# Attention scores as products of high and low parts, the rotated dimensions stacked on 128 rows

## The chip, the cores and the metric

The kernel runs on one core of a Trainium2 chip. The metric is the time of one execution in device microseconds (us). The core has a matrix engine (PE, with its weight loads PEld), a vector engine (DVE), an activation engine (ACT), a general engine (POOL), and a queue of its own for transfers (SP). Each engine works through its instructions in a fixed order and waits on semaphores for the others.

## The reference, cut to what matters

Four layers follow each other on 256 positions and 256 context positions of width 1024: a gated unit, a recurrent mixer, latent attention, and the gated unit again. The change lies in the third, the latent attention with 16 heads. A head has 128 plain dimensions and 64 rotated ones, and keys and queries are normalised over all 192:

```python
q = rms_norm((rms_norm(c_q, q_norm) @ w_uq).reshape(.., 16, 192), qk_gain_q)
k = rms_norm(concat([k_nope, broadcast(k_rope)]), qk_gain_k)      # 128 + 64
q_rot, k_rot = apply_rope(q, cos, sin), apply_rope(k, cos, sin)   # last 64 turn
s = concat([q @ k_ctx.T, q_rot @ k_rot.T])     # 256 context keys, then 256 own keys
o = softmax(s * 192 ** -0.5) @ concat([v_ctx, v])
x = x + gate * ((o * silu(z)) @ w_out)
```

So a score against a context key uses the query before its rotation, and a score against an own key the query after it.

## The kernel before, in words

Activations lie with features on the 128 partitions and positions along them. `T` is 512: context positions 0 to 255, then own positions 256 to 511.

Large products run in a one-pass format (`F32R`): each fp32 operand is split into a high part and a low part (`hi` and `lo` for weights, `x[:, 0]` and `x[:, 1]` for data), and `mm3` (L319) adds three products: high by high, high by low, low by high. A cast on ACT makes the high part (L190 and L317), a subtraction on DVE the low part (L191 and L318). Other products, the scores among them, take plain fp32 operands; the trace has two PE records for each of those.

The attention layer is the function `mla`. A scheduler sets the order on each engine; the order in which the code yields is its input.

- **Gates stage** (about 1060 to 1148 us of the span): `gates` makes 16 tiles z, one for each head; beside it run `latents` (the normalised latents, the rotated shared key `krg`) and `project(0)`.
- **Attend stage** (about 1148 to 1390 us): eight groups g of two heads each. `attend(g)` makes scores, softmax and the product with the values; `project(g+1)` runs beside it and makes the next group's keys, values and queries. From g = 5 on the first three parts of the output product run along.

In `project`, `keys` makes a head's 128 plain key rows, `scaled` multiplies them and the shared rotated key by the norm, `values` makes v, `queries` the plain query rows, `rotate` the turned query rows of both heads at once (product with a 128x128 `swap` matrix, then sine and cosine), `norms` the query norms. In `attend` a score tile `sc` of 128 queries by 512 keys takes three fp32 products (L1376 to L1378): 128 plain rows by 512 keys, 64 unrotated rows (`qo`) by the 256 context keys, 64 rotated rows (`qr`) by the 256 own keys. DVE takes the maximum, ACT the exponential, DVE scales it; PE transposes it (`pT`, L1353) half a group later and multiplies it with the values (`po`, L1358).

Weights come by `wload` (L185): a transfer into `raw`, the cast and the subtraction, with four `raw` tiles and three pairs of `hi` and `lo` in this layer.

Of the kernel before, what the change touches and what calls it, by code (L numbers as in the profile page):

```python
# [9 lines left out]
F32R = mybir.dt.float32r  # L10
AF = mybir.ActivationFunctionType
ALU = mybir.AluOpType
# [5 lines left out]
T = 512  # L18
# [18 lines left out]
def layout(inp):  # L37
# [55 lines left out]
    o["swap"] = np.kron(np.eye(2, dtype=f), sw)  # L93
# [5 lines left out]
def body(tc, I, out):  # L99
# [77 lines left out]
    def wload(src, n=None):  # L177
        return next(wparts(src, n))
# [963 lines left out]
    def mla(m):  # L1142
        with phase("2", 0, 0, 4, psum=(("pA", 4), ("pB", 4)), wn=1024, hi=3):
            ep = env["a"]

            def tl(tag, shape, bufs, dtype=F32):
                return ep.tile(list(shape), dtype, tag=tag, name=tag, bufs=bufs)
# [6 lines left out]
            swap = tl("swap", [128, 128], 1)  # L1154
# [89 lines left out]
            def rotate(dst, src):  # L1244
                p = ps("sw", "pA")
                PE.matmul(p[:, 0:256], swap, src, start=True, stop=True)
                t = tl("t1", q256, 4)
                V.tensor_tensor(t, p[:, 0:256], rope[:, 1], ALU.mult)
                V.tensor_tensor(dst, src, rope[:, 0], ALU.mult)
                V.tensor_tensor(dst, dst, t, ALU.add)  # L1250

            def project(g, d):
# [3 lines left out]
                kt = lambda: tl("hx" if g else "s", [128, T], 8 if g else 16)  # L1256
                d["krh"], d["v"] = kt(), []

                def keys(hh):
                    p = ps("kn", "pA")  # L1260
                    for k in range(2):
                        sl = slice(k * 256 + hh * 128, k * 256 + hh * 128 + 128)
                        mm3(p, w[0][:, sl], w[1][:, sl], ckv[k], k == 0, k == 1)
                    t = kt()
# [4 lines left out]
                    d["kn"].append(t)  # L1269
                    return sq  # L1270

                def scaled(hh, sq):
                    p = ps("kss", "pA")
                    PE.matmul(p, ones, sq, start=True, stop=True)
                    hf = slice(64 * hh, 64 * hh + 64)
                    r = tl("lt", [128, T], 4)
                    rsqrt_bc(r, p, 1.0 / 192, eps)
                    t = d["kn"][hh]
                    V.scalar_tensor_tensor(out=t, in0=t, scalar=vec[:, 10:11], in1=r, op0=ALU.mult, op1=ALU.mult)
                    V.tensor_tensor(d["krh"][hf], krg[hf], r[hf], ALU.mult)  # L1280
# [20 lines left out]
                scaled(0, k0)  # L1301
# [3 lines left out]
                scaled(1, k1)  # L1305
                yield
                qo, ro, qrs = tl("qo", q256, 2), tl("qr", q256, 2), tl("t1", q256, 4)
                mm256(wload(I["ml_qr"][g], 768), cq, qo)
                S.activation(qrs, qo, AF.Square)
                S.activation(qo, qo, AF.Identity, scale=vec[:, 9:10])  # L1310
                yield
                d["qo"], d["qr"], d["qn"] = qo, ro, []
                d["rq"] = rq = tl("rq", [128, 4], 2)

                def queries(hh):
                    hf = slice(64 * hh, 64 * hh + 64)
                    t = tl("qn", q256, 4)
                    mm256(wload(I["ml_qn"][g * 2 + hh], 768), cq, t)
                    sq = tl("t1", q256, 4)
                    S.activation(sq, t, AF.Square)  # L1320
                    V.tensor_tensor(sq[hf], sq[hf], qrs[hf], ALU.add)
                    S.activation(t, t, AF.Identity, scale=vec[:, 8:9])
                    d["qn"].append(t)
                    return sq
# [11 lines left out]
                rotate(ro, qo)  # L1336
                yield
                q1 = queries(1)
                norms(0, q0)
                yield  # L1340
                yield
# [24 lines left out]
            def attend(g, d, before):  # L1366

                rq = d["rq"]
                for hh in range(2):
                    hf = slice(64 * hh, 64 * hh + 64)  # L1370
                    pt = []
                    for qb in range(2):
# [3 lines left out]
                        PE.matmul(p, d["qn"][hh][:, qs], d["kn"][hh], start=True, stop=False)  # L1376
                        PE.matmul(p[:, 0:256], d["qo"][hf, qs], d["krh"][hf, 0:256], start=False, stop=False)  # L1377
                        PE.matmul(p[:, 256:512], d["qr"][hf, qs], d["krh"][hf, 256:512], start=False, stop=True)  # L1378
# [20 lines left out]
            krg = tl("krg", [128, T], 1)  # L1399

            def latents():
                yield from latent(ckvr, 6, 256, T, ckv)
                S.activation(krs, kr[0:64], AF.Square)
                S.activation(krg, kr, AF.Identity, scale=vec[:, 11:12])
                krr = tl("t1", q256, 4)
                rotate(krr, krg[:, X])
                V.tensor_copy(krg[:, X], krr)
                yield
                yield from latent(cqr, 0, 768, 256, cq)
# [67 lines left out]
```

## Time and profile before

| | |
|---|---|
| median of 3 runs | 1613.46 us (1609.02 to 1613.62) |
| profiled execution | 1612.92 us, of which the span of its instructions 1611.1 us |
| PE busy | 1519.5 us, 94% of the span |
| DVE busy | 1149.1 us, 71% |
| ACT busy | 795.2 us, 49% |

The profiled execution lies 0.54 us under the median and has 1.8 us outside its span. A share over the whole span says little here, since the four layers have different limits. How the attention layer stands is read from its own stretch: how much of it PE, DVE and ACT are busy, and whether PE had idle time there. A busy PE is not PE at its peak, because matmuls overlap; what a product costs is read from the distance between the starts of consecutive ones.

### The profile page before, as it was taken

The numbers are of one execution on the slowest core, as the hardware profiler recorded it, in microseconds if no ns is written. First come the engines' busy times: TensorE is split into PE (matmuls) and PEld (weight loads), VectorE is DVE, ScalarE is ACT, GpSimd is POOL, SyncE is SP. The second block draws the span as 40 slices with busy tenths as digits, with TensorE's granted clock in tenths as the row PEclk, the third lists the DMA queues.
The fourth block names the chain that finished last, engine by engine and source line by source line (L and its number), as shares of the span: only waits on it lengthen the run. The fifth ranks groups of instructions, "written<-read, shape, count | busy, mean of one in ns | idle before, by whom it ended". The sixth has DMA issues, their size and how long they took to land.

```text
span 1611.1 us, 29355 instructions
## 1 busy us (share of the span) xinstructions
PE 1519.5 (94%) x11860; PEld 1181.4 (73%) x11860; DVE 1149.1 (71%) x2160; ACT 795.2 (49%) x1434; POOL 101.1 (6%) x135
## 2 busy tenths in 40 slices
PE   5999999999988998999998999799999999989998
PEld 2768888888966644776776777688777777768887
DVE  3769998864898377586887844778766666665876
ACT  4534331223665354345345332569866766356543
POOL 0000000000000132303213000000000000000000
PEclk9999999999999999899999999999999999989999
DMA  9766567742144652532433133134321222265452
GB/s 352 271 246 224 191 218 260 261 153 79 53 144 150 183 164 70 153 96 74 126 99 94 62 100 121 53 118 145 115 74 53 80 85 92 70 233 199 165 183 79
DMA packets 95176, 229.07 MB, mean 142 GB/s; under 512 B 26048, under 2 KB 52160, under 8 KB 80576
## 3 DMA queue, kind: packets, MB, share of 16 engines
q1 hardware_dynamic: 92736, 223.00, 40.8%
q10 hardware_dynamic: 2304, 4.20, 0.7%
q8 instruction: 93, 1.52, 0.4%
q14 instruction: 43, 0.35, 0.1%
HBM read 208.81 MB, written 17.83 MB: 141 GB/s over the span
## 4 chain that ended last, share of the span: by engine, by line
PE 47%; DVE 7%; ACT 5%; issue 1%; POOL 1%; DMA 0%; ACTq 0%; POOLq 0%; DVEq 0%
PE fm L323 5%; PE op L323 4%; PE pg L976 3%; PE fm L324 2%; PE op L1047 2%; PE op L324 2%; PE pz L323 2%; PE pu L323 2%; PE po L1358 2%; PE sc L1376 2%; PE pe L862 2%; PE sc L1377 1%; PE pv L416 1%; PE pv L417 1%; PE pz L324 1%
## 5 line engine op out<-in xcount | busy, mean ns | idle before, releaser
L191 DVE TENSOR_TENSOR lo<-raw,hi 128x2048 fp32r<-128x2048 f32 (+3 forms) x161 | 251.7, 1567 | 108.6 <-ACT hi L190 108.1
L190 ACT CAST hi<-raw 128x2048 fp32r<-128x2048 f32 (+3 forms) x161 | 212.1, 1324 | 226.9 <-PE op L327 40.6
L258 DVE SCALAR_TENSOR_TENSOR junk<-adaw,scb 128x1024 f32<-128x1024 f32 x112 | 136.7, 1221 | 10.0 <-DMA adaw<-in_ada_wT 8.1
L323 PE MATMUL op<-s,hi 128*128 128x512 f32 x256 | 91.6, 400 | 0.0
L415 PE MATMUL pv<-hi,hp 128*128 128x512 f32 x192 | 78.2, 409 | 9.1 <-ACT hi L190 6.0
L416 PE MATMUL pv<-lo,hp 128*128 128x512 f32 x192 | 77.7, 405 | 1.7 <-DVE lo L191 1.7
L323 PE MATMUL fm<-hx,hi 128*128 128x512 f32 x200 | 74.1, 411 | 4.1 <-ACT hx L317 3.8
L417 PE MATMUL pv<-hi,hp 128*128 128x512 f32 x192 | 77.2, 402 | 0.0
L324 PE MATMUL op<-s,lo 128*128 128x256 f32 x256 | 71.1, 280 | 0.0
L976 PE MATMUL pg<-xz,wz 128*128 128x256 f32 x256 | 70.2, 408 | 0.0
L767 POOL TENSOR_TENSOR BK<-f 64x256 f32<-64x256 f32 x64 | 57.3, 895 | 44.4 <-DVE f L760 27.4
L866 DVE TENSOR_TENSOR E<-pe,masks 128x512 f32<-128x512 f32 x64 | 41.5, 682 | 25.5 <-PE pe L862 23.0
L324 PE MATMUL fm<-hx,lo 128*128 128x256 f32 x200 | 56.7, 288 | 2.0 <-DVE lo L191 2.0
L323 PEld LDWEIGHTS op<-s,hi 128*128 128x128 f32 x256 | 48.1, 188 | 12.5 <-issue 1.3
L1076 PE MATMUL pv<-wv,xv 128*128 128x512 f32 x128 | 57.2, 596 | 0.0
L1047 PE MATMUL op<-Y,wo 128*128 128x256 f32 x192 | 55.8, 427 | 1.3 <-DVE xT L1051 1.3
L323 PE MATMUL fm<-cq,hi 128*128 128x512 f32 x144 | 55.7, 422 | 0.0
L976 PEld LDWEIGHTS pg<-xz,wz 128*128 128x128 f32 x256 | 47.0, 197 | 11.5 <-issue 3.8
L415 PEld LDWEIGHTS pv<-hi,hp 128*128 128x128 f32 x192 | 37.7, 197 | 19.4 <-ACT hi L190 6.6
L326 PE MATMUL pu<-hp,hi 128*128 128x512 f32 x128 | 51.1, 400 | 0.0
L327 PE MATMUL pu<-hp,hi 128*128 128x512 f32 x128 | 50.5, 395 | 0.0
L328 PE MATMUL pz<-hp,lo 128*128 128x512 f32 x128 | 50.5, 395 | 0.0
(413 smaller groups left out, 4088.2 us busy)
## 6 DMA issues: line engine op xcount, KB each, us to landing
adaw<-in_ada_wT SPq DMA_DIRECT2D x36, 1024.0 KB, 4.9
raw<-in_sgu_v SPq DMA_DIRECT2D x16, 1024.0 KB, 4.8
raw<-in_sgu_u SPq DMA_DIRECT2D x16, 1024.0 KB, 4.8
raw<-in_sgu_z SPq DMA_DIRECT2D x16, 1024.0 KB, 4.7
raw<-in_sgu_o SPq DMA_DIRECT2D x16, 1024.0 KB, 4.8
adaw<-in_ada_w SPq DMA_DIRECT2D x24, 512.0 KB, 9.6
xz<-xz SPq DMA_DIRECT2D x32, 256.0 KB, 4.2
raw<-in_ml_z SPq DMA_DIRECT2D x16, 512.0 KB, 3.6
```

What stands on the lines that cost most here:

```text
L190: S.copy(hi[:, sl], raw[:, sl])
L191: V.tensor_tensor(lo[:, sl], raw[:, sl], hi[:, sl], ALU.subtract)
L258: V.scalar_tensor_tensor(out=junk, in0=raw[:, f, :], scalar=1.0, in1=scb[:, c, :], op0=ALU.mult, op1=ALU.mult, accum_out=m[:, t * 2 + f, c ...
L323: PE.matmul(p, whi, x, start=start, stop=False)
L324: PE.matmul(p[:, 0:256], wlo, x[:, 0], start=False, stop=stop)
L415: PE.matmul(pv[tb], hs[k][:, 0, sl], whi[:, ws_], start=k == 0, stop=False)
L416: PE.matmul(pv[tb], hs[k][:, 0, sl], wlo[:, ws_], start=False, stop=False)
L417: PE.matmul(pv[tb], hs[k][:, 1, sl], whi[:, ws_], start=False, stop=k == 7)
L767: nc.gpsimd.tensor_tensor(bk[H[h], 2 * h:2 * h + 7:2, :], k4[H[h], sg], c4[H[h], sg], ALU.mult)
L976: PE.matmul(p, ws[k // 4][:, k % 4, pr * 128:pr * 128 + 128], xs[k // 2][:, k % 2, :], start=k == 0, stop=k == 7)
L1047: PE.matmul(p[:, ob], w[:, k, ob, :], y[:, k], start=k == 0, stop=k == 1)
L1076: PE.matmul(p, xv[:, k, tb * 128:tb * 128 + 128], ws[k // 4][:, k % 4, :], start=k == 0, stop=k == 7)
```

## The change

Scores. Keys and queries of a head are kept as high and low parts, and a score tile now takes six one-pass products of 128 rows by 512 keys: three for the plain rows, three for the 64 unrotated and 64 rotated rows, which are stacked on 128 rows. For head 0 of a pair the unrotated query rows are the upper 64 and the rotated ones the lower 64; for head 1 the other way round. The key side (`krg[0]`, `krg[1]`) has zeros where an unrotated row would meet an own key or a rotated row a context key.

Rotation. `swap` becomes 128x256: its second half exchanges the two heads' rows without turning them, so that the cosine part too comes out of a product, on the rows where the stack needs it. `rotate` is now called after the second head's queries, and its result is split.

Buffers. `raw` has three tiles instead of four in this layer; the key tiles of a group are four (high and low for two heads) where they were three.

```diff
-    o["swap"] = np.kron(np.eye(2, dtype=f), sw)
+    o["swap"] = np.concatenate([np.roll(np.kron(np.eye(2, dtype=f), x), 64, 1) for x in (sw, np.eye(64, dtype=f))], 1)
...
-        with phase("2", 0, 0, 4, psum=(("pA", 4), ("pB", 4)), wn=1024, hi=3):
+        with phase("2", 0, 0, 3, psum=(("pA", 4), ("pB", 4)), wn=1024, hi=3):
...
             def rotate(dst, src):
                 p = ps("sw", "pA")
-                PE.matmul(p[:, 0:256], swap, src, start=True, stop=True)
+                for i in range(2):
+                    PE.matmul(p[:, i * 256:i * 256 + 256], swap[:, i * 128:i * 128 + 128], src, start=True, stop=True)
                 t = tl("t1", q256, 4)
                 V.tensor_tensor(t, p[:, 0:256], rope[:, 1], ALU.mult)
-                V.tensor_tensor(dst, src, rope[:, 0], ALU.mult)
-                V.tensor_tensor(dst, dst, t, ALU.add)
+                u = tl("t1", q256, 4)
+                V.tensor_tensor(u, p[:, 256:512], rope[:, 0], ALU.mult)
+                for hf, x in dst:
+                    V.tensor_tensor(x, u[hf], t[hf], ALU.add)
...
                 def scaled(hh, t, sq):
...
                     V.scalar_tensor_tensor(out=t, in0=t, scalar=vec[:, 10:11], in1=r, op0=ALU.mult, op1=ALU.mult)
-                    V.tensor_tensor(d["krh"][hf], krg[hf], r[hf], ALU.mult)
+                    x = kt(), kt()
+                    S.copy(x[0], t)
+                    V.tensor_tensor(x[1], t, x[0], ALU.subtract)
+                    d["kn"].append(x)
+                    V.tensor_tensor(r, krg[hh], r, ALU.mult)
+                    x = tl("rp", [128, 2, T], 3, F32R)
+                    split(r, x)
+                    d["kr"].append(x)
...
                 def queries(hh):
...
-                    S.activation(t, t, AF.Identity, scale=vec[:, 8:9])
-                    d["qn"].append(t)
+                    x = tl("qn", [128, 2, 256], 3, F32R)
+                    S.activation(x[:, 0], t, AF.Identity, scale=vec[:, 8:9])
+                    V.scalar_tensor_tensor(out=x[:, 1], in0=t, scalar=vec[:, 8:9], in1=x[:, 0], op0=ALU.mult, op1=ALU.subtract)
+                    d["qn"].append(x)
...
                 q0 = queries(0)
                 yield
-                rotate(ro, qo)
-                yield
+                for hh in range(2):
+                    S.copy(qo[64 * hh:64 * hh + 64, hh], qt[64 * hh:64 * hh + 64])
                 q1 = queries(1)
+                yield
                 norms(0, q0)
                 yield
+                rotate([(slice(64, 128), qo[64:128, 0]), (slice(0, 64), qo[0:64, 1])], qt)
+                d["qr"] = tl("qp", [128, 2, 2, 256], 2, F32R)
+                split(qo, d["qr"])
                 yield
                 norms(1, q1)
...
-                        PE.matmul(p, d["qn"][hh][:, qs], d["kn"][hh], start=True, stop=False)
-                        PE.matmul(p[:, 0:256], d["qo"][hf, qs], d["krh"][hf, 0:256], start=False, stop=False)
-                        PE.matmul(p[:, 256:512], d["qr"][hf, qs], d["krh"][hf, 256:512], start=False, stop=True)
+                        (kh, kl), q = d["kn"][hh], d["qn"][hh]
+                        PE.matmul(p, q[:, 0, qs], kh, start=True, stop=False)
+                        PE.matmul(p, q[:, 0, qs], kl, start=False, stop=False)
+                        PE.matmul(p, q[:, 1, qs], kh, start=False, stop=False)
+                        mm3(p, d["qr"][:, 0, hh, qs], d["qr"][:, 1, hh, qs], d["kr"][hh], False, True)
...
-                krr = tl("t1", q256, 4)
-                rotate(krr, krg[:, X])
-                V.tensor_copy(krg[:, X], krr)
+                for hh in range(2):
+                    hf, of = (slice(64 * i, 64 * i + 64) for i in (hh, 1 - hh))
+                    nc.gpsimd.memset(krg[hh][hf, X], 0.0)
+                    nc.gpsimd.memset(krg[hh][of, 0:256], 0.0)
+                    S.copy(krg[hh][hf, 0:256], kr[hf, 0:256])
+                rotate([(slice(64, 128), krg[0][64:128, X]), (slice(0, 64), krg[1][0:64, X])], kr[:, X])
```

The scheduler's order, first on PE at the end of a group's projection before the change: from the rotation of group 3 (`sw`) to the first scores that use it (`sc` from `qr`). `fm` is a query product, `kn` a key product.

```order
L1246 MATMUL sw<-qo,swap 128x256
L1353 MATMUL pT<-ident,e 128x128 x4
L323 MATMUL fm<-cq,hi 128x512
...
L324 MATMUL fm<-cq,lo 128x256
L1376 MATMUL sc<-hx,qn 128x512
L1329 MATMUL qss<-ones,t_11922 128x1 x2
L1377 MATMUL sc<-hx,qo 128x256
L1378 MATMUL sc<-hx,qr 128x256
L1358 MATMUL po<-pT,v 128x256 x4
...
L1376 MATMUL sc<-hx,qn 128x512
L1377 MATMUL sc<-hx,qo 128x256
L1378 MATMUL sc<-hx,qr 128x256
```

The same place in the changed kernel (`rp` and `qp` are the split stacked rows of keys and queries):

```order
L1249 MATMUL sw<-t_11990,swap 128x256 x2
L1374 MATMUL po<-pT,v 128x256 x4
L1392 MATMUL sc<-hx,qn 128x512
L1341 MATMUL qss<-ones,t_12088 128x1 x2
L327 MATMUL kn<-ckv,hi 128x512
...
L329 MATMUL kn<-ckv,lo 128x512
L1393 MATMUL sc<-hx,qn 128x512
L1394 MATMUL sc<-hx,qn 128x512
L327 MATMUL sc<-rp,qp 128x512
L328 MATMUL sc<-rp,qp 128x512
```

Before, a whole query product of twelve matmuls, transposes, one more score tile and a value product stand between the rotation and its first use in the next group; now a value product, two norms and one key product of six matmuls do.

On ACT, where `scaled` runs for the two heads (`lt` holds the norm), before:

```order
L286 ACTIVATE lt<-lt 128x512
L190 CAST hi<-raw 128x768
L1383 ACTIVATE e,sm<-sc,sm,rq 128x512
L1293 COPY v<-pv 128x512 x2
L317 CAST s<-z 128x256
```

and in the changed kernel (`kf` is the fp32 key, `hx` its high part):

```order
L287 ACTIVATE lt<-lt 128x512
L1283 CAST hx<-kf 128x512
L191 CAST hi<-raw 128x768
L318 CAST rp<-lt 128x512
L1302 COPY v<-pv 128x512
L1400 ACTIVATE e,sm<-sc,sm,rq 128x512
```

The cast of the scaled key stands directly behind the activation that makes the norm, with one DVE instruction between them in the data's path; the weights' cast and the exponential stand behind it.

## Rows read from the trace of the kernel before

**Rows 1.** The page's head: busy time (share of the span) of each engine.
```profile
PE 1519.5 (94%) x11860; PEld 1181.4 (73%) x11860; DVE 1149.1 (71%) x2160; ACT 795.2 (49%) x1434; POOL 101.1 (6%) x135
```
**Rows 2.** Busy time by stretch: gates stage, groups 0, 3, 5 and 7.
```profile
core 0: us, PE busy (x) PEld busy (x) DVE busy (x) ACT busy (x) POOL busy (x), PEclk, DMA share, GB/s
1090.00:1110.00 20.00, 18.29 (x102) 15.37 (x101) 19.75 (x41) 19.63 (x46) 0.00 (x0) 1.00 0.35 115
1110.00:1147.90 37.90, 37.90 (x216) 32.46 (x215) 31.67 (x57) 34.96 (x78) 0.00 (x0) 1.00 0.51 167
1147.90:1173.90 26.00, 26.00 (x128) 18.94 (x127) 18.32 (x38) 19.28 (x42) 0.00 (x0) 1.00 0.28 85
1233.20:1261.80 28.60, 28.60 (x144) 21.41 (x144) 18.17 (x38) 19.58 (x41) 0.00 (x0) 1.00 0.21 69
1288.50:1325.50 37.00, 37.00 (x191) 28.62 (x190) 24.43 (x47) 23.28 (x45) 0.00 (x0) 1.00 0.28 93
1362.60:1390.00 27.40, 27.32 (x136) 20.53 (x135) 15.18 (x35) 12.52 (x26) 0.00 (x0) 1.00 0.15 49
```
**Rows 3.** PE in order of time, a score tile and the key product behind it.
```profile
start us, us, engine line op out<-in xcount [idle before <-releaser]
1261.77 1.02 PE L1376 MATMUL sc<-hx,qn 128*128 128x512 f32 x2
...
1263.26 0.59 PE L1378 MATMUL sc<-hx,qr 64*128 64x256 f32 x2
1263.78 0.50 PE L326 MATMUL kn<-ckv,hi 128*128 128x512 f32 x1
1264.12 0.39 PE L327 MATMUL kn<-ckv,hi 128*128 128x512 f32 x1
...
1265.28 0.60 PE L1353 MATMUL pT<-ident,e 128*128 128x128 f32 x4
```
**Rows 4.** The key product's weight loads, attend stage (ns: least, median, most).
```profile
L327 PEld LDWEIGHTS kn<-ckv,hi x28: 187/188/192, 1149.2 to 1333.0; 128*128 128x128 f32 x28
```
**Rows 5.** PE in order of time, the rotation of a later group.
```profile
1281.33 0.60 PE L1246 MATMUL sw<-qo,swap 128*128 128x256 f32 x2
1281.76 0.60 PE L1353 MATMUL pT<-ident,e 128*128 128x128 f32 x4
```
**Rows 6.** ACT in order of time, gates stage.
```profile
1091.75 0.61 ACT L317 CAST ckv<-s 128x512 fp32r<-128x512 f32 x1
1092.26 0.37 ACT L1184 COPY z<-fm 128x256 f32<-128x256 f32 x1
1092.52 0.63 ACT L317 CAST ckv<-s 128x512 fp32r<-128x512 f32 x1
```
**Rows 7.** DVE in order of time, gates stage.
```profile
1094.30 0.68 DVE L318 TENSOR_TENSOR ckv<-s,ckv 128x512 fp32r<-128x512 f32 x1
1094.90 0.41 DVE L1185 TENSOR_TENSOR z<-z,fm 128x256 f32<-128x256 f32 x1
1095.23 1.22 DVE L191 TENSOR_TENSOR lo<-raw,hi 128x1024 fp32r<-128x1024 f32 x1
```
**Rows 8.** Groups of instructions, 1085 to 1390 us: ACT's waits for DVE, DVE's scaling.
```profile
L1383 ACT ACTIVATE e<-sc,sm,rq 128x512 f32<-128x512 f32 x32 | 24.8, 776 | 17.3 <-DVE sm L1381 17.3
L1309 ACT ACTIVATE t<-qo 128x256 f32<-128x256 f32 x8 | 3.3, 415 | 8.0 <-DVE qo L1185 8.0
L1320 ACT ACTIVATE t<-qn 128x256 f32<-128x256 f32 x16 | 6.7, 417 | 5.8 <-DVE qn L1185 5.8
L1279 DVE SCALAR_TENSOR_TENSOR hx<-hx,vec,lt 128x512 f32<-128x512 f32 x14 | 10.5, 752 | 18.5 <-ACT lt L286 18.2
L1280 DVE TENSOR_TENSOR hx<-krg,lt 64x512 f32<-64x512 f32 x14 | 9.6, 683 | 0.1
```
**Rows 9.** PE in order of time, the two waits in the gates stage.
```profile
1101.33 0.39 PE L324 MATMUL fm<-hx,lo 128*128 128x256 f32 x1 [0.73 <-DVE lo L191]
1105.38 0.39 PE L324 MATMUL fm<-hx,lo 128*128 128x256 f32 x1 [0.98 <-DVE lo L191]
```
**Rows 10.** Weight transfers of the gates stage.
```profile
DMA to landing us min/median/max: 2.9/3.5/4.7
```

More of the change, by code (lines that the diff above doesn't have):

```diff
@@ L1153, in mla @@
             nc.sync.dma_start(out=rope, in_=I["rope"])
-            swap = tl("swap", [128, 128], 1)
+            swap = tl("swap", [128, 256], 1)
             nc.sync.dma_start(out=swap, in_=I["swap"])
@@ L1255, in project @@
                 d["kn"] = []
-                kt = lambda: tl("hx" if g else "s", [128, T], 8 if g else 16)
-                d["krh"], d["v"] = kt(), []
+                kt = lambda: tl("hx" if g else "s", [128, T], 8 if g else 16, F32R)
+                d["kr"], d["v"] = [], []
                 def keys(hh):
@@ L1263, in keys @@
                         mm3(p, w[0][:, sl], w[1][:, sl], ckv[k], k == 0, k == 1)
-                    t = kt()
+                    t = tl("kf", [128, T], 2)
                     S.copy(t, p)
@@ L1268, in keys, with scaled @@
                     V.tensor_tensor(sq[0:64], sq[0:64], krs, ALU.add)
-                    d["kn"].append(t)
-                    return sq
-                def scaled(hh, sq):
+                    return t, sq
+                def scaled(hh, t, sq):
                     p = ps("kss", "pA")
                     PE.matmul(p, ones, sq, start=True, stop=True)
-                    hf = slice(64 * hh, 64 * hh + 64)
                     r = tl("lt", [128, T], 4)
                     rsqrt_bc(r, p, 1.0 / 192, eps)
-                    t = d["kn"][hh]
                     V.scalar_tensor_tensor(out=t, in0=t, scalar=vec[:, 10:11], in1=r, op0=ALU.mult, op1=ALU.mult)
-                    V.tensor_tensor(d["krh"][hf], krg[hf], r[hf], ALU.mult)
+                    x = kt(), kt()
[6 more added lines that the diff above has]
+                    d["kr"].append(x)
                 def values(tb):
@@ L1300, in project @@
                 yield
-                scaled(0, k0)
+                scaled(0, *k0)
                 yield
@@ L1304, in project @@
                 yield
-                scaled(1, k1)
+                scaled(1, *k1)
                 yield
[L1307 to L1310, printed above, removed]
+                qo, qrs, qt = tl("qo", [128, 2, 256], 1), tl("t1", q256, 4), tl("t1", q256, 4)
+                mm256(wload(I["ml_qr"][g], 768), cq, qt)
+                S.activation(qrs, qt, AF.Square)
+                S.activation(qt, qt, AF.Identity, scale=vec[:, 9:10])
                 yield
-                d["qo"], d["qr"], d["qn"] = qo, ro, []
+                d["qn"] = []
                 d["rq"] = rq = tl("rq", [128, 4], 2)
@@ L1316, in queries @@
                     hf = slice(64 * hh, 64 * hh + 64)
-                    t = tl("qn", q256, 4)
+                    t = tl("qf", q256, 2)
                     mm256(wload(I["ml_qn"][g * 2 + hh], 768), cq, t)
@@ L1335, in project @@
                 yield
-                rotate(ro, qo)
+                for hh in range(2):
+                    S.copy(qo[64 * hh:64 * hh + 64, hh], qt[64 * hh:64 * hh + 64])
+                q1 = queries(1)
                 yield
-                q1 = queries(1)
                 norms(0, q0)
                 yield
+                rotate([(slice(64, 128), qo[64:128, 0]), (slice(0, 64), qo[0:64, 1])], qt)
+                d["qr"] = tl("qp", [128, 2, 2, 256], 2, F32R)
+                split(qo, d["qr"])
                 yield
@@ L1369, in attend @@
                 for hh in range(2):
-                    hf = slice(64 * hh, 64 * hh + 64)
                     pt = []
@@ L1398, in mla @@
             krs = tl("krs", [64, T], 1)
-            krg = tl("krg", [128, T], 1)
+            krg = [tl(f"krg{hh}", [128, T], 1) for hh in range(2)]
             def latents():
@@ L1403, in latents @@
                 S.activation(krs, kr[0:64], AF.Square)
-                S.activation(krg, kr, AF.Identity, scale=vec[:, 11:12])
-                krr = tl("t1", q256, 4)
-                rotate(krr, krg[:, X])
-                V.tensor_copy(krg[:, X], krr)
+                S.activation(kr, kr, AF.Identity, scale=vec[:, 11:12])
+                for hh in range(2):
[4 more added lines that the diff above has]
+                rotate([(slice(64, 128), krg[0][64:128, X]), (slice(0, 64), krg[1][0:64, X])], kr[:, X])
                 yield
```

## The prediction

> **What bounds the kernel now.** I read the head of the page first: PE is busy 94% of the span, but a busy PE is not yet a PE at its peak [rows 1]. So I read the attention layer by stretches. In the attend stage PE has no idle time: 26.00 of 26.00 us in group 0, 28.60 of 28.60 in group 3, 37.00 of 37.00 in group 5, 27.32 of 27.40 in the last group, while ACT and DVE are busy for 63 to 74% up to group 5 and less in the last [rows 2]. The granted clock is 1.00 in all these stretches, the level of 2.4 GHz, so no clock effect is in play. There a microsecond taken from PE is a microsecond of time, as long as ACT and DVE keep up. The gates stage is different: from 1090 to 1110 us ACT is busy 19.63 of 20 us and DVE 19.75, and PE stands still for 1.71 us [rows 2], in two waits for the low part of a weight tile, 0.73 and 0.98 us [rows 9]. There added ACT or DVE work is paid. From 1110 to 1148 us ACT is busy 34.96 of 37.90 us, 92%, and PE again has no idle time [rows 2]: that is as full as an engine beside PE has been seen here without costing anything.
>
> **Scores.** The cost on PE is the distance of starts. The score tile starts at 1261.77 us; the products behind it are evenly spaced only from 1264.12 on, and from there five one-pass products of 512 keys take 1.16 us to 1265.28, 0.232 us each [rows 3]. The first of them began therefore at 1263.89 in effect, so a score tile costs 2.12 us. (Its recorded start at 1263.78 would make 2.01; 0.11 us is lost in passing from the products with 64 rows to those with 128.) The new tile is six one-pass products of the same shape, 6 x 0.232 = 1.39 us. The gain is 0.73 us, 32 times (the 32 exponentials are one for each tile [rows 8]): 23.2 us. With 2.01 it would be 19.8 us, which is the lower bound; since the new tile has 128 rows throughout I see nothing that would keep the 0.11 us, and take 23.2.
>
> **Rotation.** A product with `swap` takes 0.43 us on PE, 1281.33 to 1281.76 [rows 5]. A second one is added in each of nine rotations: +3.9 us, of which 3.0 in the seven that run in the attend stage and 0.9 in the gates stage. PE alone is thus 23.2 - 3.9 = 19.3 us shorter, 20.2 in the attend stage.
>
> **What ACT and DVE get.** For each group with a projection, ACT gets five casts of 512 columns (two for the scaled plain keys, two for the stacked keys, one for the stacked queries) and two copies of 256 columns. Back to back a cast of 512 takes 0.51 us from start to start and a copy of 256 columns 0.26 [rows 6]; together 3.1 us (by their full durations, 0.61 to 0.63 and 0.37, 3.8). DVE gets five subtractions of 512 columns, one instruction more in the rotation and two for the low parts of the queries. Back to back these take 0.60 and 0.33 us [rows 7], together 4.0 us (by durations, 0.68 and 0.41, 4.6). On DVE half the partitions do not make an instruction shorter: 64x512 takes 0.683 us [rows 8], 128x512 0.68 [rows 7]. So I count a 64x256 one as a 128x256 one, on ACT too. Casting queries straight out of the scaling costs nothing: that ACT instruction was there.
>
> Group 3 then has PE 28.6 - 4 x 0.73 + 0.43 = 26.1 us, ACT 19.58 + 3.1 = 22.7 (87% of it) and DVE 18.17 + 4.0 = 22.2 (85%): under the 92% that cost nothing. Group 5 has PE 34.5 us, ACT 26.4, DVE 28.4. Group 0 is the tight one: PE 26.0 - 2.5 = 23.5 us, ACT 22.4 and DVE 22.3, 95% each. The last group projects nothing and simply gains.
>
> **Waits that are new.** In `scaled`, the cast of the key stands directly behind the norm's activation on ACT and needs one DVE instruction of 0.75 us in between [rows 8]; twice a group ACT stands for at least that long, with the weights' cast and an exponential queued behind it, and PE waits for both of these. At the end of a group the first scores of the next one need the split stacked queries. Between the rotation and that use PE has a value product (eight passes of about 0.215, half of 0.43 [rows 5]: 1.7 us), six key products and three plain score products (9 x 0.232 = 2.1), together 3.8 us. The path beside it is two DVE products and two additions (4 x 0.33), the cast 0.51 to 0.61 on ACT, for the last product also a subtraction (0.60), plus whatever stands between them on DVE: 1.9 to 3.8 us. The cover just suffices. Price of both kinds of wait: 0 to about 2 us a group. Nearest is the stretch with ACT at 92% and no loss, so I take a quarter, 0.5 us, in six groups, and 1 us in group 0: 4 us.
>
> **Gates stage.** ACT gets group 0's 3.1 us and two copies for the shared key, 0.5; DVE 4 us. ACT's sum over 1090 to 1148 us is 19.63 + 34.96 + 3.6 = 58.2 us, where the stretch is now 57.9 long. At 98%, what ACT reached in its fullest part, that takes 59.4. The cost lies between PE's own 0.9 us and 4.5 (all of ACT's 3.6 and the 0.9); I take 2.2, a little over the 1.5 that the 98% gives.
>
> **Cheap edits.** Three raw tiles instead of four: a transfer is issued when the subtraction three tiles back is done instead of four, and lands 3.5 us later [rows 10]; a z tile's sixteen products, eight of 512 columns at 0.232 us [rows 3] and eight of 256 at an estimated half of that, keep PE for 2.8 us, so three tiles cover 8.4. Cost 0, at most some 0.4 us once or twice in the gates stage. The four memsets run on POOL, which is otherwise idle there [rows 2]. The swap matrix is loaded early; its second half is 64 KB. Up to this layer every engine's order is the same as before, apart from the line numbers.
>
> **Sum.** -20.2 (attend stage, PE) + 4 (waits there) + 2.2 (gates stage) = -14.0 us on the profiled execution's 1612.92: 1598.9, so I say 1599. That execution lies 0.5 us under the median of the runs shown, whose spread is 4.6 us.
>
> **One rule against the change.** Rows: weight loads of 0.188 us [rows 4] stand beside products 0.232 us apart [rows 3], so a load is hidden behind the product before it although both use all 128 rows. The Trainium skill, page "TensorE: Matmul & The Clock Gate", section "The mechanism" in its Part 3, says that weight loads overlap with running matmuls only when they go to different row groups. By that rule the loads of the new tile would stand between its products; the trace here contradicts it. As a mechanism it is the last rival below.
>
> **Rivals.**
> 1. No wait at all: PE's sum alone, -19.3 us, 1593.6. For it: no idle PE in any group today [rows 2]. Against it: the gates stage already loses 1.71 us [rows 9].
> 2. The waits take most of the gain: 1.5 us in each of the seven groups (the split queries late by what stands between on DVE, and ACT standing at the scaled keys), gates stage 4.5. -20.2 + 10.5 + 4.5 = -5.2 us, 1607.7. For it: two casts a group whose input is one DVE instruction old; group 0 at 95%. Against it: that ACT and DVE still have 13% and 15% to spare in group 3.
> 3. Slower: ACT in its fixed order becomes the bound. ACT's 22.7 us in group 3, plus the waits for DVE that it has today, (17.3 + 8.0 + 5.8) / 8 = 3.9 us a group [rows 8], plus the new ones, 2 x 0.75 and 4 x 0.33 = 2.8, make 29.4 us against 28.6 today. With 0.8 us lost in seven groups, 4.5 in the gates stage and 2.9 gained in the last group that is +7.2 us, 1620. It decides from the point where that cycle passes 28.6 us, that is, if today's waits stay when ACT falls behind. Against it: from 1090 to 1110 us, where ACT was behind, it stood still for 0.37 us in 20 [rows 2]; an engine that is behind finds its inputs ready.
> 4. Loads not hidden: six products with their loads take 6 x (0.188 + 0.232) = 2.52 us instead of 2.12 [rows 3, 4]. 32 x 0.40 + 3.9 = +16.7 us, 1630. Against it: the spacing just named.
>
> **How the numbers follow.** Chances: the forecast 0.60 (by itself 1595 to 1603), rival 1 0.10, rival 2 0.22, rival 3 0.06, rival 4 0.02. A measurement of this kernel can tell about 0.3%, 5 us, from no change: faster is below 1608.6, slower above 1618.3. Faster: 0.60 + 0.10 and two thirds of rival 2, 0.84. Same: the rest of rival 2 and a little of rival 3, 0.09. Slower 0.07. The range goes from 1593, rival 1 with no wait, to 1608, which takes in half of rival 2.
>
> **What would show it.** In the changed profile, starts of the six products of a score tile 0.23 us apart and the tile 1.4 us long: right; 0.4 us apart: rival 4. Groups like group 3 every 26 to 27 us, with PE idle under 1 us in each, ACT near 87% and DVE near 85%: right. PE waiting for the products from `qp` at the start of a group, or for weight casts, 1.5 us or more a group: rival 2. ACT at 95% in every group and groups of 28.6 us or longer: rival 3. The stretch of the gates stage 1 to 4 us longer, with the waits still for low parts of weights. The forecast is wrong if the attend stage is shorter by under 10 us, or if another layer's time moves by more than a microsecond or two.

## The result, and the profile after

The changed kernel takes 1596.53 us (median of 4 runs, 1589.95 to 1600.94) and the kernel before 1613.54 us (4 runs, 1609.02 to 1615.99): a ratio of 0.990, with a 95% interval from 0.9877 to 0.9922. Forecast were 1599, with a range from 1593 to 1608. A later repetition with 6 and 11 runs gave 1595.26 against 1609.38 us, ratio 0.9904 (0.9887 to 0.9922).

The profiled execution of the changed kernel is its fastest, 1589.95 us. The head of its page, which answers to [rows 1]:

```profile
span 1588.2 us, 29464 instructions
PE 1498.7 (94%) x11878; PEld 1188.0 (75%) x11878; DVE 1177.7 (74%) x2224; ACT 817.1 (51%) x1492; POOL 101.7 (6%) x139
```

PE's busy time fell by 20.8 us, with 18 instructions more; DVE's and ACT's rose by 28.6 and 21.9. The span fell by 22.9 us, more than the sum of -14.0 could explain. To see how much of that is the attention layer, one needs a mark at both ends of it. I take the first product of the layer's input norm (`ssq`) and the same product of the next layer. Of the kernel before, PE in order of time:

```profile
1041.40 1.76 PE L290 MATMUL ssq<-acc,ones 128*128 128x512 f32 x2 [3.06 <-DVE acc L279]
...
1410.04 0.85 PE L290 MATMUL ssq<-acc,ones 128*128 128x256 f32 x2 [2.15 <-DVE acc L279]
```

The same two of the changed kernel:

```profile
1034.62 1.24 PE L291 MATMUL ssq<-acc,ones 128*128 128x512 f32 x2 [3.06 <-DVE acc L280]
...
1387.52 0.67 PE L291 MATMUL ssq<-acc,ones 128*128 128x256 f32 x2 [2.15 <-DVE acc L280]
```

From mark to mark the layer took 368.64 us and takes 352.90: -15.74. Another 6.78 us of the span were gone before the layer began, in layers that the change doesn't touch, and 0.4 after it. This stretch, "the layer" from here on, is the measure of the experiments. Within it the part up to the first score product went from 106.54 to 109.72 us and the part behind it from 262.10 to 243.18.

Busy time by stretch, columns as in [rows 2]: the gates stage, then groups 0, 3, 5 and 7.

```profile
1090.00:1110.00 20.00, 18.15 (x98) 14.98 (x97) 19.56 (x43) 19.22 (x45) 0.00 (x0) 1.00 0.52 168
1110.00:1148.00 38.00, 38.00 (x220) 32.83 (x219) 32.40 (x58) 36.85 (x85) 0.00 (x0) 1.00 0.52 161
1144.30:1168.20 23.90, 23.89 (x129) 19.87 (x128) 21.84 (x49) 21.77 (x51) 0.00 (x0) 1.00 0.26 76
1219.90:1246.40 26.50, 26.50 (x146) 22.27 (x145) 21.59 (x47) 22.20 (x49) 0.00 (x0) 1.00 0.20 65
1273.10:1309.70 36.60, 36.60 (x204) 31.41 (x203) 30.02 (x60) 27.09 (x56) 0.00 (x0) 1.00 0.30 90
1343.00:1367.50 24.50, 24.30 (x133) 20.67 (x133) 16.12 (x39) 12.54 (x27) 0.00 (x0) 1.00 0.21 66
```

PE still has hardly any idle time in the attend stage. Group 3 takes 26.50 us where it took 28.60, with ACT busy 84% of it and DVE 81%; group 0 takes 23.9, with both at 91%. From 1110 to 1148 us ACT is now at 97%, and PE still doesn't stand there. (The layer began 6.8 us earlier, so the first two windows hold somewhat later work than those of [rows 2].) Group 5 took 36.60 us where 34.5 was expected, but its window now holds six key products and a norm product that stood in the next group's window before: groups 5 and 6 together went from 74.1 to 69.9 us, -4.2, where twice the 2.5 us of group 5 were expected.

A score tile that one-pass products follow, PE in order of time; it answers to [rows 3]:

```profile
1152.25 0.39 PE L1392 MATMUL sc<-s,qn 128*128 128x512 f32 x1
1152.48 0.39 PE L1393 MATMUL sc<-s,qn 128*128 128x512 f32 x1
...
1153.41 0.39 PE L329 MATMUL sc<-rp,qp 128*128 128x512 f32 x1
1153.64 1.02 PE L1278 MATMUL kss<-lt,ones 128*128 128x512 f32 x2
```

From 1152.25 to 1153.64 it is 1.39 us, as predicted from six times 0.232. And the rotation of group 3's projection, which answers to [rows 5]:

```profile
1243.91 1.11 PE L1249 MATMUL sw<-t,swap 128*128 128x256 f32 x4
1244.86 1.89 PE L1374 MATMUL po<-pT,v 128*128 128x256 f32 x8
```

Two fp32 products (four records) take 0.95 us from start to start, where 2 x 0.43 was expected.

The last group has no projection beside it and no new split, so it shows best what a score tile gives by itself. Its first product before, and in the changed kernel with the norm product ahead of it:

```profile
1362.56 1.02 PE L1376 MATMUL sc<-hx,qn 128*128 128x512 f32 x2
```

```profile
1342.62 0.50 PE L1341 MATMUL qss<-ones,t 128*128 128x1 f32 x4
1342.98 0.48 PE L1392 MATMUL sc<-hx,qn 128*128 128x512 f32 x1
1343.30 0.40 PE L1393 MATMUL sc<-hx,qn 128*128 128x512 f32 x1
```

From the first score product to the layer's end it is 47.48 us before and 44.54 after, 2.94 less. Of this 0.43 us is the norm product, which stood behind that first score product before. The rest, 2.5 us for four tiles, is 0.63 us a tile.

The waits of the attend stage (engine and what waits, what it waits for, us in total, times, the longest), the lines that matter here:

```profile
ACT e L1400 <- DVE sm L1398: 7.8, 7, 2.0
ACT hx L1283 <- DVE kf L1281: 5.6, 7, 1.0
PEld qss L1341 <- DVE t L1331: 2.6, 5, 0.7
PEld sc L327 <- ACT qp L318: 0.4, 2, 0.2
PEld sc L329 <- DVE qp L319: 0.3, 1, 0.3
```

ACT's wait for the maxima fell from 17.3 us [rows 8] to 7.8; the cast of the scaled key brought the new 5.6. The largest wait on PE's side is that of the weight loads of `qss`, the product of the query norms, for DVE's sum of squares. The last two lines are the seam: first scores that wait for the split stacked queries, 0.7 us in all.

### The profile page after: what moved, and what is told of

Its sections match the earlier page's. It is cut to its first block, busy times and chain, and to the rows that moved or that the text cites. A ratio compares the mean times of both kernels' runs of the same rounds, so it can differ in the third digit from the quotient of the medians.

```text
span 1588.2 us, 29464 instructions
## 1 busy us (share of the span) xinstructions
PE 1498.7 (94%) x11878; PEld 1188.0 (75%) x11878; DVE 1177.7 (74%) x2224; ACT 817.1 (51%) x1492; POOL 101.7 (6%) x139
## 4 chain that ended last, share of the span: by engine, by line
PE 44%; ACT 7%; DVE 6%; issue 1%; DMA 1%; POOL 1%; SPq 0%; ACTq 0%; DVEq 0%; POOLq 0%
PE fm L324 4%; PE op L324 4%; PE pg L977 3%; PE fm L325 2%; PE op L1048 2%; PE op L325 2%; PE pz L324 2%; PE pu L324 2%; PE pe L863 2%; PE po L1374 2%; PE pv L417 1%; PE pv L418 1%; PE pz L325 1%; PE pu L325 1%; PE pv L416 1%
## 5 line engine op out<-in xcount | busy, mean ns | idle before, releaser
L1048 PE MATMUL op<-Y,wo 128*128 128x256 f32 x192 | 51.2, 399 | 1.3 <-DVE xT L1052 1.3
```

The costliest lines, as they stand in the source:

```text
L1048: PE.matmul(p[:, ob], w[:, k, ob, :], y[:, k], start=k == 0, stop=k == 1)
```

## The experiments

Layer, its two parts and the whole time, in us. "Up to scores" runs from the layer's mark to the first score product, and where it ends depends on the order, so single parts compare only between kernels with the same products ahead of it: before, e1 and e5; after, e2, e3 and e11; e7, e9, e10 and e12; e4 and e8. "Before beside it" is the kernel before on the same chip.

| run | layer | up to scores | from scores on | time | before beside it |
|---|---|---|---|---|---|
| before | 368.64 | 106.54 | 262.10 | 1612.92 | |
| after | 352.90 | 109.72 | 243.18 | 1589.95 | 1613.54 |
| e1_plain_only | 364.36 | 106.29 | 258.08 | 1605.31 | 1607.04 |
| e2_stacked_only | 356.00 | 109.22 | 246.79 | 1594.53 | 1607.04 |
| e3_splits_twice | 357.61 | 111.95 | 245.66 | 1602.44 | 1607.04 |
| e4_rot_onepass | 352.63 | 104.85 | 247.78 | 1602.61 | 1607.04 |
| e5_before_raw3 | 368.71 | 106.62 | 262.10 | 1610.47 | 1611.72 |
| e6_rot_early | 352.58 | 105.22 | 247.35 | 1600.63 | 1611.72 |
| e7_norms_late | 350.94 | 108.20 | 242.74 | 1592.15 | 1611.72 |
| e8_norms_late_onepass | 353.18 | 104.83 | 248.35 | 1594.91 | 1611.72 |
| e9_norms_late_pool | 349.79 | 107.26 | 242.53 | 1591.63 | 1614.17 |
| e10_norms_late_onepass_pool | 348.42 | 107.99 | 240.43 | 1585.86 | 1614.17 |
| e11_after_again | 352.62 | 109.50 | 243.12 | 1595.26 (6 runs) | 1609.38 (11 runs) |
| e12_best | 349.84 | 109.39 | 240.45 | 1588.99 (5 runs) | 1609.38 (11 runs) |

The same kernel twice gave 352.90 and 352.62 (after, e11) and 348.42 and 349.84 (e10, e12). Differences of the layer under about 1.5 us are therefore not read as effects. This scatter lies ahead of the first score: from scores on, where the granted clock is 1.00 in every profile, the same code repeats within 0.1 us (262.10 twice for before and e5, 243.18 and 243.12 for after and e11, 240.43 and 240.45 for e10 and e12). The times of single runs tell less still: runs of one kernel scatter by 5 to 11 us, mostly from outside the layer.

**e1_plain_only.** From the kernel before: only the plain rows are split; the rotated rows keep their two fp32 products of 64 rows, and there is one rotation product. It has three `raw` tiles, as the changed kernel (e5 tests that by itself).

```diff
...
-  PE.matmul(p, d["qn"][hh][:, qs], d["kn"][hh], start=True, stop=False)
+  (kh, kl), q = d["kn"][hh], d["qn"][hh]
+  PE.matmul(p, q[:, 0, qs], kh, start=True, stop=False)
+  PE.matmul(p, q[:, 0, qs], kl, start=False, stop=False)
+  PE.matmul(p, q[:, 1, qs], kh, start=False, stop=False)
```

> Before, with only the plain 128 rows of keys and queries in high and low parts; the 64 unrotated and 64 rotated rows stay fp32 products of 64 rows, one rotation product, three raw tiles. The measure is the layer's stretch, from its first norm product (ssq) to the next layer's: 368.6 us before, 352.9 in the changed kernel. Theory (PE is the bound, each score tile costs what its products cost): the plain part falls from 0.86 to 0.70 us, 0.16 us x 32 = 5.1 us, less about 1 us of waits: layer 364 to 365 us. Rival (the plain part carries most of the gain, because fp32 passes are what was dear): layer below 360 us.

The layer is 4.28 us shorter, as the theory has it: one fp32 product of 512 columns is replaced by three one-pass ones, which saves little each time.

**e2_stacked_only.** From the changed kernel: only the rotated rows are split and stacked, with the second rotation product; the plain rows stay one fp32 product.

```diff
...
-  (kh, kl), q = d["kn"][hh], d["qn"][hh]
-  PE.matmul(p, q[:, 0, qs], kh, start=True, stop=False)
-  PE.matmul(p, q[:, 0, qs], kl, start=False, stop=False)
-  PE.matmul(p, q[:, 1, qs], kh, start=False, stop=False)
+  PE.matmul(p, d["qn"][hh][:, qs], d["kn"][hh], start=True, stop=False)
```

> The changed kernel with the plain rows as one fp32 product again; stacked rows in parts, two rotation products. Theory: the 64-row part falls from 1.26 us (with 0.2 us of passing to 64 rows and back) to 0.70, 0.56 x 32 = 17.9 us, less 3.9 for the rotation and about 2 for the gates stage and waits: layer 356 to 357 us. With e1 the two gains add up to the whole (15.7 us) within 2 us. Rival (gains don't add, since waits of ACT and DVE take what PE gives): layer at or under 354 us, the plain part adding nothing.

The layer is 12.64 us shorter than before: this half is three quarters of the gain, although it carries the rotation's cost. e1 and e2 together make 16.9, the whole 15.7; the two halves add, within what can be told. The second half does two things at once, stacking on 128 rows and splitting, and no run separates them. By the rows' prices, as an estimate: an fp32 product of 512 columns at 2 x 0.43 = 0.86 us [rows 5] leaves 2.12 - 0.86 = 1.26 us a tile for the two products of 64 rows; stacking alone would make that 0.86, splitting then 0.70.

**e3_splits_twice.** The new splits are each done twice on ACT and DVE (plain keys, stacked keys, stacked queries); PE's products are the same, some in another order.

```diff
+  S.copy(x[0], t)
   S.copy(x[0], t)
   V.tensor_tensor(x[1], t, x[0], ALU.subtract)
+  V.tensor_tensor(x[1], t, x[0], ALU.subtract)
...
+  S.copy(x[:, 0], r)
   split(r, x)
+  V.tensor_tensor(x[:, 1], r, x[:, 0], ALU.subtract)
...
+  S.copy(d["qr"][:, 0], qo)
   split(qo, d["qr"])
+  V.tensor_tensor(d["qr"][:, 1], qo, d["qr"][:, 0], ALU.subtract)
```

> The changed kernel with each new split done twice into the same place: 5 casts more on ACT and 5 subtractions more on DVE in each group (2.6 and 3.0 us). Theory (PE is the bound, ACT and DVE have about 15% to spare in most groups): ACT and DVE near 93 to 95% of group 3, the attend stage 1 to 4 us longer, the gates stage 2 to 3; layer 355 to 359 us. Rival (ACT or DVE already set the pace): about 3 us in each of eight groups, layer 374 us or more.

The layer is 4.7 us longer than after, in the range of the theory; a layer bound by ACT and DVE would have been far longer (rival). Half of it falls ahead of the scores (2.2 us), half behind (2.5). So even the second set of splits costs little, which makes it likely, though no run shows it, that the first cost no more; and doubling them shows where they press first. PE in order of time, rows with an idle time before them:

```profile
1226.25 0.61 PE L1345 MATMUL qss<-ones,t 128*128 128x1 f32 x4 [0.81 <-DVE t L1335]
...
1253.84 0.61 PE L1345 MATMUL qss<-ones,t 128*128 128x1 f32 x4 [1.13 <-DVE t L1335]
...
1281.41 0.61 PE L1345 MATMUL qss<-ones,t 128*128 128x1 f32 x4 [1.09 <-DVE t L1335]
```

It is the product of the query norms, the place of the small wait of after, and neither the scaled keys nor the seam to the next group.

**e4_rot_onepass.** The rotation's products become one-pass: the queries before the rotation are split, and each half of `swap` (exact in one part) is multiplied with the high and the low part.

```diff
...
+  xs = tl("kf", [128, 2, 256], 2, F32R)
+  split(src, xs)
   for i in range(2):
-      PE.matmul(p[:, i * 256:i * 256 + 256], swap[:, i * 128:i * 128 + 128], src, start=True, stop=True)
+      for j in range(2):
+          PE.matmul(p[:, i * 256:i * 256 + 256], swap[:, i * 128:i * 128 + 128], xs[:, j], start=j == 0, stop=j == 1)
```

> The changed kernel with the rotation in the one-pass format: its source is split, four products of 256 columns of one pass instead of two fp32 products; one cast (0.3 us on ACT) and one subtraction (0.33 on DVE) more in each group. Theory (PE is the bound): a rotation costs 0.46 instead of 0.87 us on PE, nine times: layer 3 to 3.7 us shorter, 349 to 350 us. Rival (ACT and DVE set the pace, or the path from rotation to scores does): no gain, 352.9 or longer.

A miss: 352.63, no gain over after. PE's starts of `sw` do lie closer (5.77 us over the layer instead of 7.83), but PE waits more in return. Its weight loads in the attend stage:

```profile
PEld qss L1346 <- DVE t L1336: 3.3, 7, 0.7
...
PEld po L1379 <- ACT pT L1375: 1.2, 3, 0.5
```

Together these are 4.5 us where after has 2.9 in the same two waits (2.6 and 0.3): the split that makes the rotation cheap for PE loads DVE and ACT in the very place where PE already waits for them.

**e5_before_raw3.** The kernel before with three `raw` tiles instead of four.

```diff
-  with phase("2", 0, 0, 4, psum=(("pA", 4), ("pB", 4)), wn=1024, hi=3):
+  with phase("2", 0, 0, 3, psum=(("pA", 4), ("pB", 4)), wn=1024, hi=3):
```

> The kernel before with three raw tiles in the attention layer instead of four, nothing else. Theory (a transfer lands 3.5 us after its issue, the tiles in hand cover 8.4 us): layer stretch 368.6 us as before, within 1 us. Rival (the prefetch is too short, and part of what the gates stage lost in the changed kernel is this): gates stage 1.3 us or more longer.

368.71 against 368.64: the buffer costs nothing in the kernel before. (The opposite, four tiles in the changed kernel, wasn't run.)

**e6_rot_early.** Rotation and split right behind the first head's queries, ahead of the second's.

```diff
   for hh in range(2):
       S.copy(qo[64 * hh:64 * hh + 64, hh], qt[64 * hh:64 * hh + 64])
+  rotate(...); d["qr"] = tl("qp", ...); split(qo, d["qr"])
   q1 = queries(1)
   yield
   norms(0, q0)
   yield
-  rotate(...); d["qr"] = tl("qp", ...); split(qo, d["qr"])
```

> The changed kernel with the rotation and its split called right behind the first head's queries, ahead of the second head's query product. It tells whether the seam (first scores of a group waiting for the split stacked queries) costs anything in the changed kernel. Theory (no: PE's waits there are for the norms' squares): layer 352 to 354 us. Rival (the late rotation costs 0.5 us or more a group): layer 349 us or less.

352.58, no gain. This alone doesn't clear the seam, because the edit brings a new wait, at the rotation's own weight loads, which want the tile that ACT has just made:

```profile
PEld sw L1249 <- ACT t L1320: 2.9, 7, 0.5
```

That the seam costs little is read from the trace of after instead: 0.7 us of waits in all.

**e7_norms_late.** The first head's norm product moves behind the rotation; so DVE has longer for its sum of squares.

```diff
-  norms(0, q0)
-  yield
   rotate(...); d["qr"] = tl("qp", ...); split(qo, d["qr"])
   yield
+  norms(0, q0)
+  yield
   norms(1, q1)
```

> The changed kernel with the first head's norm product (qss) called one step later, behind the rotation instead of ahead of it. In the changed kernel's trace PE waits at qss for DVE's sum of squares, 2.6 us in five waits. Theory (these are the waits that are left, and moving the product behind other PE work hides them): layer 1 to 2.5 us shorter, 350.5 to 352 us. Rival (the wait moves to another instruction, since DVE is behind): 352.9 or longer.

350.94 (-1.7 to -2.0 against the two profiles of after). Of the 2.6 us of `qss` this is left:

```profile
PEld qss L1341 <- DVE t L1331: 0.3, 1, 0.3
```

The gain lies where the wait lay. Six key products (1.48 us) that stand ahead of the first score in after stand behind it in e7; with them counted alike, e7 is 1.9 us shorter from scores on (242.74 - 1.48 = 241.26 against 243.18) and unchanged ahead of them. That speaks for most of the wait at `qss` having been paid; but the edit also gives the rotation other neighbours, and no run separates the two.

**e8_norms_late_onepass.** e7 with the rotation of e4.

> The changed kernel with both the one-pass rotation of e4 and the later norm product of e7. In e4 PE's rotation was 2.1 us shorter, but qss took 1.3 us more, and the layer only 0.3 less. Theory (the gain of e4 was given back at qss, so it shows once qss is hidden): layer 2 us or more under that of e7, 348.5 to 350 us. Rival (ACT and DVE, which e4 loads with a cast and a subtraction more a group, hold the stage): as e7 or longer.

A miss in the other direction: 353.18, 2.2 us longer than e7, with PE idle 4.0 us from the scores on. PE in order of time, two of three such places:

```profile
1220.41 0.70 PE L1379 MATMUL po<-pT,v 128*128 128x256 f32 x2 [1.00 <-ACT pT L1375]
...
1247.48 0.70 PE L1379 MATMUL po<-pT,v 128*128 128x256 f32 x2 [1.00 <-ACT pT L1375]
```

The value product waits for ACT to copy the transposed weights; its weight loads in the whole stage:

```profile
PEld po L1379 <- ACT pT L1375: 4.8, 4, 1.6
```

ACT in order of time ahead of the first place:

```profile
1218.54 0.51 ACT L1338 ACTIVATE qn<-qf,vec 128x256 fp32r<-128x256 f32 x1
1219.08 0.40 ACT L1354 COPY qo<-t 64x256 f32<-64x256 f32 x1
1219.50 0.37 ACT L1187 COPY qf<-fm 128x256 f32<-128x256 f32 x1
1219.77 0.59 ACT L1375 COPY pT<-pT 128x512 f32<-128x512 f32 x1
1220.39 0.41 ACT L318 CAST kf<-t 128x256 fp32r<-128x256 f32 x1
```

ACT has no gap there; the copy of `pT` is simply late in its fixed order, behind small copies. So in this order of work ACT is what the cheaper rotation runs into.

**e9_norms_late_pool.** e7 with the small copies (two to `qo` in each group, two to `krg`) moved from ACT to POOL.

```diff
-  S.copy(qo[64 * hh:64 * hh + 64, hh], qt[64 * hh:64 * hh + 64])
+  nc.gpsimd.tensor_copy(qo[64 * hh:64 * hh + 64, hh], qt[64 * hh:64 * hh + 64])
...
-  S.copy(krg[hh][hf, 0:256], kr[hf, 0:256])
+  nc.gpsimd.tensor_copy(krg[hh][hf, 0:256], kr[hf, 0:256])
```

> e7 (later norm product) with the copies of unrotated rows, two in each group (0.40 us each on ACT) and two for the shared key, moved from ACT to POOL, which is idle in this layer. Theory (ACT is the engine beside PE that is nearest its limit: 98% in the gates stage): gates stage about 1 us shorter, attend stage unchanged, layer 349.5 to 350.5 us. Rival (ACT isn't what PE waits for, or POOL's copy is so slow that the stacked queries come late): 351 us or longer.

349.79, as expected, though 1.15 us less than e7 is inside the scatter: 0.94 of it lies ahead of the scores, 0.2 behind. The groups of POOL's instructions in this kernel (busy us, mean ns, idle time before):

```profile
L1349 POOL COPY qo<-t 64x256 f32<-64x256 f32 x16 | 6.8, 423 | 243.2 <-ACT t L1320 242.8
```

and the same group on ACT in after:

```profile
L1349 ACT COPY qo<-t 64x256 f32<-64x256 f32 x16 | 6.5, 404 | 0.2
```

POOL, idle anyway, needs 0.42 us for what ACT does in 0.40.

**e10_norms_late_onepass_pool.** e8 with the copies on POOL.

> e8 (later norm product and one-pass rotation) with the same copies on POOL. In e8 PE waited 4.8 us for ACT's copies of the transposed scores. Theory (ACT's work is what took e8's gain): those waits fall by half or more, layer 349 to 351 us, against 353.2 in e8. Rival (the waits come from the order on ACT, not from how much it has to do): 352.5 us or longer.

348.42, 4.8 us less than e8 and 4.5 less than after. The waits of the value product for ACT have shrunk from 4.8 us in four weight loads (e8) to this:

```profile
PEld po L1379 <- ACT pT L1375: 0.3, 1, 0.3
```

With 18 copies off ACT the loss of e8 is gone. The edit also changes the scheduler's order on PE: at the first place shown for e8 the value product that waits stands right behind a score tile, with the rotation behind it; in e10 the rotation stands ahead of that tile. So whether ACT's load or its new order took the waits away isn't separated.

What the cheaper rotation gains is read against e9, which has the copies on POOL and the fp32 rotation. From scores on it's 2.1 us (242.53 to 240.43, and 240.45 in e12), clear of the scatter there; ahead of the scores it costs 0.7 us (2.1 in e12). Over the layer that leaves 1.4 us, and nothing in e12, which is inside the scatter.

**e11_after_again.** The changed kernel once more, for the scatter and beside e12.

> The changed kernel once more, with five rounds against the kernel before on the same chip. Theory (the layer alone changed): layer stretch 352.9 us within 1 us, the other layers scattered by several us as between all runs so far, the time 14 to 18 us under before, ratio 0.989 to 0.992. Rival (part of the gain is in the earlier layers, which were 6.8 us shorter in its first profile): the earlier layers again under those of every other kernel here, ratio under 0.988.

The layer repeats within 0.3 us, while its start, at 1034.62 us in the first profile, is at 1037.80 here. The median, -14.1 us against the kernel before, and the first, -17.0, lie on either side of the layer's -15.7.

**e12_best.** e10, timed.

> The kernel of e10 (later norm product, one-pass rotation, copies on POOL), timed in five rounds beside e11. Theory (its layer stretch is 348.4 us against 352.9): 4 to 5 us faster than e11, ratio to before 0.986 to 0.989. Rival (a scatter of several us in other layers hides it): the same as e11 within its interval.

1588.99 us (1585.84 to 1595.03), ratio 0.9871 with an interval from 0.9851 to 0.9891: faster than both kernels by the medians, 6.3 us below e11 on the same chip, somewhat more than expected. The two ratios' intervals still touch (0.9887 to 0.9891); the layer's 348.4 and 349.8 against 352.6 and 352.9 speaks for a true gain of 2.8 to 4.5 us.

## Why the prediction came out right, step by step

- **PE bounds the attend stage, and what is taken from PE is gained.** Right. Its parts need one correction: with the new order six key products (1.48 us) and a norm product (0.37) that used to stand behind the first score now stand ahead of it, 1.85 us. The attend stage proper is then -18.92 + 1.85 = -17.1 us; -16.2 was predicted.
- **Scores, 0.73 us each, 23.2 in all.** The new tile is right, 1.39 us, but the gain was put too high where it can be seen by itself: 0.63 us a tile in the last group, near the 0.62 that the prediction had as its lower bound. The sum agrees: 17.1 us net and 3.0 for the rotations at the predicted price are 20.1, or 0.63 a tile, if no waits are counted. With the 2.6 us of the `qss` waits counted it is 0.71; which holds in the groups with a projection isn't separated. The prediction saw nothing that would keep the 0.11 us, which it read as the price of passing from 64 to 128 rows. The last group has the same delay without any product of 64 rows: the first one-pass product behind the fp32 norm product takes 0.32 us (1342.98 to 1343.30) instead of 0.23. So it belongs to the passing from fp32 to one-pass products too, and the changed kernel still has such places. e1 and e2 show where the gain comes from: 4.3 us from the plain rows, 12.6 from the stacked ones with their rotations.
- **Rotation, +3.9.** About right: PE's starts of `sw` cover 3.36 us before and 7.83 after over the layer, +4.5, or 0.50 for each of the nine instead of 0.43. In e7, where other products stand behind them, the same rotations cover 6.47, +3.1.
- **What ACT and DVE get.** Right for group 3 (84% and 81%, predicted 87 and 85), and in group 0 both are at 91% where 95 was predicted. That they could take it is shown by PE's own time: from the scores to the layer's end it stood idle for 2.9 us, of which 2.15 is the wait at the end mark, against 2.2 before.
- **New waits, 4 us.** The place was wrong, and the size at most about right. PE waits about 2.6 us at `qss`, for DVE's squares and sums of the queries, a place that the prediction doesn't name. At the seam to the next group, which it does name, the waits are 0.7 us in all, and ACT's wait at the scaled key (5.6 us in total, at most 1.0) is absorbed. e7 removes the wait at `qss` and gains 1.7 to 2.0 us. So the scores gave up to 3 us less than forecast and the waits took up to 4 us less; that the stage's sum came out within 1 us is partly luck.
- **Gates stage, +2.2.** Raw +3.18; less the 1.85 of moved work it is +1.3, of which 0.8 is the two rotations (their starts cover 0.78 us before and 1.54 after). PE's idle time from the layer's mark to the first score rose from 6.17 to 6.43 us only. ACT came close to the 98% that it was allowed: 97% from 1110 to 1148 us.
- **Raw tiles, 0.** Right (e5).
- **Rival 3** needed ACT's waits of today to remain. They didn't: 17.3 us of waiting for maxima became 7.8, as is to be expected of an engine that falls behind and finds its inputs ready. **Rival 2** needed 1.5 us in each group; all of PE's idle time from the scores on is 0.8 us, beside the 2.6 of the weight loads. **Rival 4** asked for loads that stand between the products; the six products start 0.23 us apart. The sentence of the Trainium skill, page "TensorE: Matmul & The Clock Gate", Part 3, "The mechanism", that loads overlap only across row groups, is contradicted by this trace as well.
- **One sign was read too strictly.** The prediction called itself wrong if another layer moved by more than a microsecond or two. The earlier layers moved by 6.8 us in the profiled execution, but the same kernel run twice moves there as much (below). The layer's own stretch, not the span, is what had to be compared: with nothing but the layer changed, the profiled execution would have come to 1612.92 - 15.74 = 1597.2 us. Its 1589.95 lies under the range because of the other layers.

Whether the 2.6 us of the weight loads and the 0.8 us of idle time are wholly separate isn't settled: two of the idle times (0.32 and 0.22 us) are at the same `qss`.

## What to carry to other kernels

Where PE is busy all the time, price a change by the distance between PE's starts, in a stretch between two marks that the change doesn't touch, best one whose granted clock stays at 1.00; the span also holds the scatter of everything else. Here the fp32 products on 64 rows were the first to convert: the two of a tile, stacked on 128 rows and split, gave most of the gain, while splitting the full one brought a quarter. Work that is taken from PE by giving ACT or DVE a split paid here only where these engines were not late at that place: find the product that waits for them, give it distance or move small copies to an idle engine, and then try the same edit again, as in e4, e8 and e10.

## What the runs showed of the hardware that was not expected

**Part of the scatter goes with the granted clock of earlier layers.** e10 and e12 are the same kernel. The layer began at 1035.30 us in one and at 1041.75 in the other. The stretch from 600 to 800 us, first e10, columns as in [rows 2]:

```profile
600.00:800.00 200.00, 180.75 (x2747) 132.03 (x2747) 148.19 (x338) 87.60 (x173) 50.39 (x56) 0.94 0.35 105
```

and e12:

```profile
600.00:800.00 200.00, 181.99 (x2704) 132.44 (x2702) 146.18 (x329) 86.97 (x171) 50.30 (x56) 0.91 0.35 103
```

In the same 200 us, at a granted clock of 0.91 instead of 0.94, PE got through 43 products fewer in e12 (2704 against 2747), some 3 us at this rate, and 6.5 us is what the layer began later. More was lost between 840 and 965 us, where the clock was 1.00 in e10 and 0.97 in e12; that the clock accounts for all of it isn't shown. In all profiles of the study the layer began between 1034.6 and 1047.9 us. Within the layer the clock is under 1.00 at its start in every profile (its mean up to the scores is 0.94 to 0.96) and 1.00 from the scores on. e12 has one more place, in the gates stage:

```profile
1100.00:1107.00 7.00, 5.35 (x21) 4.28 (x21) 6.22 (x14) 5.36 (x14) 0.00 (x0) 0.76 0.27 81
```

A mean of 0.76 over 7 us is some 3.4 us at the lower level (1.2 GHz); PE was busy for 5.35 of these 7 us. It stands beside e12's gates stage being 1.4 us longer than e10's.
